# Mixer C's row of scores as one PSUM tile over three banks: one minimum and one exponential for all its keys

## The chip, the cores and the metric

The kernel runs on one core of one Trainium2 chip, as one launch. Its time is the device time of that core in microseconds (us); the figure that counts is the median of the timed runs. A core has TensorE (PE, matrix products into PSUM; loads of its weights are listed apart as PEld), VectorE (DVE), ScalarE (ACT) and GpSimd (POOL) as computing engines, and DMA queues, most of which are fed from SyncE (SP). Each engine takes its instructions in its own order; between engines they wait on semaphores. PSUM is TensorE's output memory, here eight banks of 512 float32 values on each of 128 partitions.

## The reference

The program is one step of a network with two layers over 128 context tokens and 1024 latent tokens, all in float32. The change is in the second layer, whose mixer C is differential attention: each of 8 heads has two query/key maps (z = 0 and 1) of width 64 and values of width 128. A softmax is taken over each map, and the second one, times a number lam, is taken from the first:

```python
def diff_attn_latent(q, k, v, k_ctx, v_ctx, lam):
    ...
    k_all = jnp.concatenate([k_ctx, k], 1)
    v_all = jnp.concatenate([v_ctx, v], 1)
    ...
    def one_block(qblk):
        s = jnp.einsum('bqhzd,bkhzd->bhzqk', qblk, k_all, preferred_element_type=F32) * (C_QK_DIM ** -0.5)
        p = jax.nn.softmax(s, -1)
        att = p[:, :, 0] - lam * p[:, :, 1]
        return jnp.einsum('bhqk,bkhd->bqhd', att.astype(v.dtype), v_all)
```

A latent query block of 128 tokens sees 128 cached context keys and 1024 latent keys, 1152 in all. The 128 context tokens of the other input see one another only: 128 keys. The result goes through a norm, a gate and the output projection.

## The kernel before

Tokens are in nine tiles of 128: tile 0 is the context tokens, tiles 1 to 8 the latent ones. Each float32 operand of most products is split into a high and a low part (hh and hl, wch and wcl, vh and vl, ah and al), and a product is made of two or three matmuls of those parts.

For a head h and a query tile t, `c_probs` (L1539) works on the two maps in turn, and each map's 128 x 1152 scores are called a row of scores here. It makes six matmuls (L1555): three chunks of 384 keys, each a high and a low part of the query. Every chunk has a PSUM tile of its own, one bank, with the tags s0, s1 and s2. VectorE takes each chunk's minimum (the query is scaled by -1/8, so the least value is the largest score; L1557) and the minimum of the three (L1559). ScalarE makes three exponentials with that as bias, each of which also gives the sum over its chunk (L1562; the sum is read by an instruction of its own, ACTIVATION_READ_ACCUMULATOR). After both maps L1571 adds up the three sums, L1573 and L1574 make the factor, and L1575 mixes the two rows into the attention. Tile 0 has one chunk of 128 keys. Between the maps `c_query` (L1528) transposes and splits the next tile's queries.

`c_values` (L1579) later transposes the attention by blocks of 128 keys (L1593), splits it into ah (ScalarE, L1438) and al (VectorE, L1439), and multiplies it with the values (L1603 to L1605).

PSUM is full: two banks each for the pools cpr (projections and gates, tag ps) and ctr (transposes, tag pt), three for csc (the scores, one buffer for each of s0, s1 and s2) and one for cpo (value products). So a chunk's matmuls of the next row can begin when that chunk's exponential of the row before has read its bank. At the end, the output tiles 3, 5 and 7 borrow s0 and s1 as their two banks (p_b, L1851).

What order the work stands in is set in two steps. The program interleaves generators: for every head, rows of scores, value products, the projections of the next head (L360 to L362, `c_project`), gates (L1620 to L1622, `c_gate`) and norms (`c_norm`) are zipped by counts of steps (L1797 and L1804 to L1807). From that a scheduler makes each engine's list by its own estimates of when operands and buffers are free, so a change of instructions also moves others. In the lists a row of scores has the number of its tile (s_19111).

Of the kernel before, what the change touches and what calls it, by code (L numbers as in the profile page):

```python
# [13 lines left out]
AF = mybir.ActivationFunctionType  # L14
ALU = mybir.AluOpType
AX = mybir.AxisListType
# [3 lines left out]
P = 128  # L20
# [3 lines left out]
TOK = NT * P  # L24
# [117 lines left out]
def hybrid_step(ctx: ExitStack, tc: tile.TileContext, I, O, stop=99):  # L142
    nc = tc.nc
    PE, VE, AE, GE, SP = nc.tensor, nc.vector, nc.scalar, nc.gpsimd, nc.sync
# [12 lines left out]
    def tl(pool, shape, tag, dt=F32, bufs=None):  # L157
        uid[0] += 1
        kw = {} if bufs is None else {"bufs": bufs}
        return pool.tile(list(shape), dt, tag=tag, name=f"{tag}_{uid[0]}", **kw)  # L160
# [534 lines left out]
    with ExitStack() as ph1:  # L695
        hp = ph1.enter_context(space("hT0", 1))
        hh, hl = tl(hp, [P, KT, TOK], "hh", F32R), tl(hp, [P, KT, TOK], "hl", F32R)
        with ExitStack() as su:
# [28 lines left out]
            for i in range(3):  # L727
                modulated(i, range(4, KT), thirds[i], xp, pt, hh, hl)
        ap = ph1.enter_context(space("ap", 1))
# [4 lines left out]
        psum = [ph1.enter_context(space(n, b, space=PSUM))  # L734
                for n, b in (("psc", 2), ("ppo", 1), ("ptr", 3), ("ppr", 2))]
        psum = psum[3], psum[2], psum[0], psum[1]
# [535 lines left out]
    with ExitStack() as ph2:  # L1272
# [96 lines left out]
        for i in range(-2, len(items)):  # L1369
# [47 lines left out]
            t = TIMES[min(i + 2, 2) if i < 5 else 3]  # L1417
# [121 lines left out]
    def c_probs(h, t, heads, ap, psum):  # L1539

        p_pr, p_tr, p_s, p_o = psum
        own = t == 0
        nb, w = (1, P) if own else (3, THIRD)
        hd = heads[h]
        if t not in hd.qs:
            c_query(t, hd, ap, psum)
        qs = hd.qs[t]
        p = []
        sums = tl(ap, [P, 2, nb], f"cs{nb}")
        for z in range(2):  # L1550
            s = [tl(p_s, [P, 512], f"s{c}") for c in range(nb)]
            mc, mx = tl(ap, [P, 3], "mc3"), tl(ap, [P, 1], "mx")
            for c in range(nb):
                for e in range(2):
                    PE.matmul(s[c][:, :w], qs[:, e, z], hd.kp[:, z] if own else hd.kst[:, z, w * c:w * c + w],  # L1555
                              start=e == 0, stop=e == 1)
                VE.tensor_reduce(mc[:, c:c + 1] if nb > 1 else mx, s[c][:, :w], axis=AX.X, op=ALU.min)  # L1557
            if nb > 1:
                VE.tensor_reduce(mx, mc, axis=AX.X, op=ALU.min)  # L1559
            e = tl(ap, [P, TOK], "p", bufs=4)  # L1560
            for c in range(nb):
                AE.activation(e[:, w * c:w * c + w], s[c][:, :w], AF.Exp, scale=-1.0, bias=mx,  # L1562
                              accum_out=sums[:, z, c:c + 1])
            p.append(e[:, :nb * w])
            if z == 0:
                h1, t1 = (h, t + 1) if t < 8 else (h + 1, 0)
                if h1 < 8 and t1 in heads[h1].q:
                    c_query(t1, heads[h1], ap, psum)
            yield
        li = hd.sums[:, 2 * t:2 * t + 2]  # L1570
        VE.reduce_sum(li, sums, axis=AX.X)  # L1571
        r = tl(ap, [P, 1], "lr")
        VE.reciprocal(r, li[:, 1:2])  # L1573
        VE.scalar_tensor_tensor(r, r, nlam, li[:, 0:1], op0=ALU.mult, op1=ALU.mult)  # L1574
        VE.scalar_tensor_tensor(p[0], p[1], r, p[0], op0=ALU.mult, op1=ALU.add)  # L1575
        hd.att[t] = p[0]
        yield
# [102 lines left out]
    with ExitStack() as ph3:  # L1680
# [76 lines left out]
        if stop <= 3:  # L1757
# [3 lines left out]
        ap = ph3.enter_context(space("ac", 2))  # L1761
        psum = [ph3.enter_context(space(n, b, space=PSUM))
                for n, b in (("cpr", 2), ("ctr", 2), ("csc", 1), ("cpo", 1))]
# [84 lines left out]
                yield  # L1848

        p_a = lambda: [tl(psum[0], [P, 512], "ps") for _ in range(2)]  # L1850
        p_b = lambda: [tl(psum[2], [P, 512], f"s{i}") for i in range(2)]  # L1851
        banks = [p_a, p_a]

        def first_ready():
# [33 lines left out]
```

## Time and profile before

| | us |
|---|---|
| time, median of 3 runs | 2082.01 |
| lowest and highest run | 2075.63 and 2087.13 |
| span of the profiled execution | 2077.4 |
| scores of mixer C, first to last | 1181 to 1998 |
| six score matmuls of a row, 128 such rows (L1555, 1152 keys) | 196.0 busy |
| chunk minima (L1557, 384 keys) | 204.4 busy |
| exponentials (L1562, those of tile 0 among them) | 225.1 busy |

The page gives the profiled execution's span, from its first to its last instruction, and no device time beside it; the span lies within the range of the three timed runs, 4.6 us below their median. The page has each engine's busy time with its share of the span and its instructions. A window gives the same for a stretch of time, with TensorE's granted clock (PEclk, 1.00 is full). A group's row has the line, the engine, the operation, output<-inputs, the shapes and the count; then the busy time, the mean of one in ns, and the idle time of the engine just before them with what ended it. A row of the waits says who waited for whom, for how long in all, how many times and at most. A row of the timeline has the start, the duration and the instruction, with the idle time ahead of it in brackets.

### The profile page before, as it was taken

What the parts mean: (1) busy time and instruction counts of PE and PEld (TensorE: products, weight loads), DVE (VectorE), ACT (ScalarE), POOL (GpSimd) and SP (SyncE); (2) the same over time, 40 slices, a digit from 0 to 9 for tenths busy, and PEclk for the clock granted to TensorE, in tenths of its full rate; (3) what the DMA queues carried; (4) which work ended last, traced back from release to release, by engine and by line L of the source; (5) the groups of instructions that cost most, each with busy time, mean ns of one, the idle gap of its engine ahead of it and who ended that gap; (6) DMA issues with size and microseconds to landing.
All of it is one profiled execution on the core that took longest, in us unless ns stands there. A gap on an engine that the chain in (4) does not pass through costs nothing. (4 is left out here: it accounts for less than half of the span.)

```text
span 2077.4 us, 40804 instructions
## 1 busy us (share of the span) xinstructions
PE 1952.1 (94%) x15148; PEld 1777.4 (86%) x15148; DVE 1488.3 (72%) x3821; ACT 1058.8 (51%) x2808; POOL 673.6 (32%) x951
## 2 busy tenths in 40 slices
PE   7899999999789999999989999999999999999998
PEld 7899999999678888777768888999998989898786
DVE  5355567565767787877488587878787878787867
ACT  4343345333446555564356554565555555555643
POOL 0222232332167657575043223121312121212204
PEclk9999999999999999999999999999999999999999
DMA  7511133112555454534576401010101010101325
GB/s 290 163 62 65 61 98 115 63 57 78 181 178 158 146 171 148 157 111 129 167 228 218 133 21 45 15 50 10 51 9 55 6 56 5 55 5 49 106 68 177
DMA packets 165079, 205.72 MB, mean 99 GB/s; under 512 B 16368, under 2 KB 108048, under 8 KB 164880
## 3 DMA queue, kind: packets, MB, share of 16 engines
q1 hardware_dynamic: 162016, 198.25, 30.1%
q10 hardware_dynamic: 2864, 4.85, 0.7%
q8 instruction: 120, 1.97, 0.4%
q14 instruction: 79, 0.65, 0.1%
HBM read 152.32 MB, written 50.74 MB: 98 GB/s over the span
## 5 line engine op out<-in xcount | busy, mean ns | idle before, releaser
L1562 ACT ACTIVATE p<-s,mx 128x384 f32<-128x384 f32 (+1 forms) x400 | 225.1, 572 | 123.0 <-DVE mx L1559 100.3
L1557 DVE TENSOR_REDUCE mc<-s 128x1 f32<-128x384 f32 x384 | 204.4, 551 | 29.3 <-PE s L1555 26.2
L1555 PE MATMUL s<-kst,qs 128*128 128x384 f32 x768 | 196.0, 355 | 14.1 <-ACT p L1562 13.6
L360 PE MATMUL ps<-wch,hh 128*128 128x384 f32 x576 | 205.5, 358 | 3.0 <-DMA raw<-in_wgc_dram 0.9
L361 PE MATMUL ps<-wcl,hh 128*128 128x384 f32 x576 | 198.6, 345 | 4.1 <-POOL wcl L271 4.1
L362 PE MATMUL ps<-wch,hl 128*128 128x384 f32 x576 | 196.4, 341 | 0.3 <-DVE hl L1707 0.2
L407 POOL TENSOR_TENSOR q<-ropea,ropeb 128x256 f32<-128x256 f32 x56 | 44.0, 786 | 442.4 <-DVE ropeb L404 302.3
L374 PE MATMUL ps<-hh,wgh 128*128 128x384 f32 x504 | 174.5, 346 | 5.8 <-DVE bo L242 4.3
L376 PE MATMUL ps<-hh,wgl 128*128 128x384 f32 x504 | 172.4, 342 | 0.0
L375 PE MATMUL ps<-hl,wgh 128*128 128x384 f32 x504 | 171.9, 341 | 0.0
L1555 PEld LDWEIGHTS s<-kst,qs 128*128 128x128 f32 x768 | 127.5, 190 | 29.8 <-ACT p L1562 22.4
L271 POOL TENSOR_TENSOR wgl<-raw,wgh 128x1024 fp32r<-128x1024 f32 (+1 forms) x39 | 75.5, 1939 | 234.5 <-ACT wgh L270 234.5
L1083 POOL TENSOR_TENSOR rp<-rp,tmp 128x126 f32<-128x126 f32 (+22 forms) x279 | 130.3, 467 | 21.9
L1081 POOL TENSOR_TENSOR tmp<-mp,rp 128x126 f32<-128x126 f32 (+22 forms) x279 | 117.8, 422 | 52.3 <-DVE mp L1072 31.1
L1438 ACT CAST ah<-pt 128x512 fp32r<-128x512 f32 (+2 forms) x168 | 86.1, 533 | 79.7 <-PE pt L1593 76.3
L1439 DVE TENSOR_TENSOR al<-pt,ah 128x512 fp32r<-128x512 f32 (+2 forms) x168 | 100.6, 615 | 32.1 <-ACT ah L1438 30.8
L360 PEld LDWEIGHTS ps<-wch,hh 128*128 128x128 f32 x576 | 109.6, 191 | 6.5 <-DVE vl L1439 2.4
L361 PEld LDWEIGHTS ps<-wcl,hh 128*128 128x128 f32 x576 | 109.8, 191 | 6.2 <-POOL wcl L271 5.8
L362 PEld LDWEIGHTS ps<-wch,hl 128*128 128x128 f32 x576 | 109.5, 190 | 1.4 <-DVE hl L1707 1.3
L271 POOL TENSOR_TENSOR wcl<-raw,wch 128x512 fp32r<-128x512 f32 x54 | 76.5, 1423 | 84.5 <-ACT wch L270 84.5
L374 PEld LDWEIGHTS ps<-hh,wgh 128*128 128x128 f32 x504 | 95.4, 189 | 8.1 <-DVE bo L242 4.9
L1575 DVE SCALAR_TENSOR_TENSOR p<-p,lr,p 128x1152 f32<-128x1152 f32 (+1 forms) x72 | 98.4, 1367 | 0.4
(463 smaller groups left out, 5721.7 us busy)
## 6 DMA issues: line engine op xcount, KB each, us to landing
hb<-pbT SPq DMA_DIRECT2D x90, 256.0 KB, 3.9
adaw<-in_ada_w_dram SPq DMA_DIRECT2D x56, 256.0 KB, 3.6
raw<-in_wc_dram SPq DMA_DIRECT2D x48, 256.0 KB, 2.7
adaw<-in_ada_w_dram SPq DMA_DIRECT2D x8, 1024.0 KB, 10.9
pbT<-bm SPq DMA_DIRECT2D x16, 512.0 KB, 2.7
low<-lowT SPq DMA_DIRECT2D x16, 512.0 KB, 4.1
raw<-in_wo_dram SPq DMA_DIRECT2D x32, 256.0 KB, 2.8
raw<-in_wpb_dram SPq DMA_DIRECT2D x13, 512.0 KB, 3.4
```

The lines of the kernel that those rows point to most:

```text
L271: eng.tensor_tensor(lo[:, j:j + w], raw[:, :w], hi[:, j:j + w].bitcast(F32), ALU.subtract)
L360: PE.matmul(ps[:, :n], hh[:, k, s], wh[:, k], start=k == 0, stop=False)
L361: PE.matmul(ps[:, :n], hh[:, k, s], wl[:, k], start=False, stop=False)
L362: PE.matmul(ps[:, :n], hl[:, k, s], wh[:, k], start=False, stop=k == KT - 1)
L374: PE.matmul(ps[:, :THIRD], wh[:, k], hh[:, k, s], start=k == 0, stop=False)
L375: PE.matmul(ps[:, :THIRD], wh[:, k], hl[:, k, s], start=False, stop=False)
L376: PE.matmul(ps[:, :THIRD], wl[:, k], hh[:, k, s], start=False, stop=k == KT - 1)
L1081: eng.tensor_tensor(tv, m[:, j - a:j - a + 1, 0:j].to_broadcast([P, n, j]), rpb[:, t:16, j:j + 1].to_broadcast([P, n, j]), ALU.mult)
L1083: eng.tensor_tensor(rpb[:, t:16, 0:j], rpb[:, t:16, 0:j], tv, ALU.add)
L1555: PE.matmul(s[c][:, :w], qs[:, e, z], hd.kp[:, z] if own else hd.kst[:, z, w * c:w * c + w], start=e == 0, stop=e == 1)
L1557: VE.tensor_reduce(mc[:, c:c + 1] if nb > 1 else mx, s[c][:, :w], axis=AX.X, op=ALU.min)
L1562: AE.activation(e[:, w * c:w * c + w], s[c][:, :w], AF.Exp, scale=-1.0, bias=mx, accum_out=sums[:, z, c:c + 1])
```

## The change

The three chunks of a row become one tile of three banks, [128, 3, 512], of which 384 columns of each bank are used. The six matmuls write its banks as before. One minimum over both free dimensions takes the place of the three chunk minima and the minimum of them, one exponential over all 1152 keys takes the place of three, and its sum goes straight into the array of sums, so L1571 is gone. The pool keeps its three banks and one buffer, so the next row's first matmul now follows the whole exponential of the row before. Tile 0's rows take the first 128 columns of such a tile. The output tiles that borrowed s0 and s1 take the first two banks of one such tile.

```diff
-        sums = tl(ap, [P, 2, nb], f"cs{nb}")
+        li = hd.sums[:, 2 * t:2 * t + 2]
         for z in range(2):
-            s = [tl(p_s, [P, 512], f"s{c}") for c in range(nb)]
-            mc, mx = tl(ap, [P, 3], "mc3"), tl(ap, [P, 1], "mx")
+            s, mx = tl(p_s, [P, 3, 512], "s"), tl(ap, [P, 1], "mx")
+            sv = s[:, 0:nb, 0:w]
             for c in range(nb):
                 for e in range(2):
-                    PE.matmul(s[c][:, :w], qs[:, e, z], hd.kp[:, z] if own else hd.kst[:, z, w * c:w * c + w],
+                    PE.matmul(sv[:, c], qs[:, e, z], hd.kp[:, z] if own else hd.kst[:, z, w * c:w * c + w],
                               start=e == 0, stop=e == 1)
-                VE.tensor_reduce(mc[:, c:c + 1] if nb > 1 else mx, s[c][:, :w], axis=AX.X, op=ALU.min)
-            if nb > 1:
-                VE.tensor_reduce(mx, mc, axis=AX.X, op=ALU.min)
-            e = tl(ap, [P, TOK], "p", bufs=4)
-            for c in range(nb):
-                AE.activation(e[:, w * c:w * c + w], s[c][:, :w], AF.Exp, scale=-1.0, bias=mx,
-                              accum_out=sums[:, z, c:c + 1])
-            p.append(e[:, :nb * w])
+            VE.tensor_reduce(mx, sv, axis=AX.XY, op=ALU.min)
+            e = tl(ap, [P, TOK], "p", bufs=4)[:, :nb * w]
+            AE.activation(e.rearrange("p (c n) -> p c n", n=w), sv, AF.Exp, scale=-1.0, bias=mx,
+                          accum_out=li[:, z:z + 1])
+            p.append(e)
...
-        li = hd.sums[:, 2 * t:2 * t + 2]
-        VE.reduce_sum(li, sums, axis=AX.X)
...
-        p_b = lambda: [tl(psum[2], [P, 512], f"s{i}") for i in range(2)]
+        p_b = lambda: [v for v in [tl(psum[2], [P, 3, 512], "s")] for v in (v[:, 0], v[:, 1])]
```

The file is five lines shorter, so lines behind `c_probs` have lower numbers after it: the mixing is L1575 before and L1570 in the change, the gates are L1615 to L1617.

The first place shown is TensorE's list in a middle head, from one row of scores (query tile 2, z = 0) to the next (z = 1). Names are output<-inputs: s is a row of scores, ps a projection or a gate, pt a transpose; x2 is two in a row. Before:

```order
L1555 MATMUL s_3853_19726<-kst_18062,qs_19652 128x384 x2
...
L1555 MATMUL s_3854_19727<-kst_18062,qs_19652 128x384 x2
...
L1555 MATMUL s_3855_19728<-kst_18062,qs_19652 128x384 x2
L362 MATMUL ps_19781<-wch_19375,hl_12965 128x384
...
L1519 MATMUL pt_19805<-cst_61,k_19752 128x128 x2
L1658 MATMUL pt_19810<-cst_61,sq_19677 128x128 x2
L1555 MATMUL s_3865_19762<-kst_18062,qs_19652 128x384 x2
```

And in the change, between the same two rows:

```order
L1555 MATMUL s_19111<-kst_17618,qs_19047 128x384 x6
L360 MATMUL ps_19150<-wch_18783,hh_12964 128x384
...
L1519 MATMUL pt_19173<-cst_61,k_19129 128x128 x2
L1653 MATMUL pt_19178<-cst_61,sq_19072 128x128 x3
...
L1588 MATMUL pt_19199<-cst_61,p_19042 128x128
L1615 MATMUL ps_19223<-hh_12964,wgh_19188 128x384
...
L1555 MATMUL s_19139<-kst_17618,qs_19047 128x384 x6
```

The six matmuls of a row now stand together, where others stood among them before. From the last of one row to the first of the next there were seven projection matmuls and four transposes; now there are twelve projection matmuls, three of a gate and six transposes.

The second place is VectorE's list at the same point, where mc and mx are the minima, lr the factor of the mixing and p the attention. Before:

```order
L1557 TENSOR_REDUCE mc_3856_19729<-s_3854_19727 128x1
L1571 TENSOR_REDUCE sums_18063<-cs_3831_19629 128x2
L1439 TENSOR_TENSOR vl_19404<-ps_19615,vh_19403 128x128
L1573 RECIPROCAL lr_19705<-sums_18063 128x1
L1557 TENSOR_REDUCE mc_3856_19729<-s_3855_19728 128x1
L1574 SCALAR_TENSOR_TENSOR lr_19705<-lr_19705,nlam_5651,sums_18063 128x1
L1559 TENSOR_REDUCE mx_19730<-mc_3856_19729 128x1
L1575 SCALAR_TENSOR_TENSOR p_19645<-p_19697,lr_19705,p_19645 128x1152
```

And in the change:

```order
L1568 RECIPROCAL lr_19091<-sums_17619 128x1
L1569 SCALAR_TENSOR_TENSOR lr_19091<-lr_19091,nlam_5651,sums_17619 128x1
L1570 SCALAR_TENSOR_TENSOR p_19042<-p_19086,lr_19091,p_19042 128x1152
L1557 TENSOR_REDUCE mx_19112<-s_19111 128x1
L1439 TENSOR_TENSOR vl_18812<-ps_19019,vh_18811 128x128
```

The mixing of the tile before stood behind the new row's minimum of three (L1559); in the change it stands ahead of the new row's one minimum.

## The prediction

> **What bounds the kernel now.** I read the page first, then the windows of the part that the change touches, then the waits of TensorE.
>
> ```profile
> span 2077.4 us, 40804 instructions
> PE 1952.1 (94%) x15148; PEld 1777.4 (86%) x15148; DVE 1488.3 (72%) x3821; ACT 1058.8 (51%) x2808; POOL 673.6 (32%) x951
> ...
> core 0: us, PE busy (x) PEld busy (x) DVE busy (x) ACT busy (x) POOL busy (x), PEclk, DMA share, GB/s
> 1182.00:2000.00 818.00, 785.93 (x4870) 728.80 (x4871) 649.33 (x1801) 467.65 (x1387) 190.09 (x184) 0.99 0.12 36
> ...
> 1538.78:1641.83 103.05, 100.03 (x636) 93.92 (x636) 82.34 (x234) 58.42 (x176) 24.03 (x25) 1.00 0.10 31
> 1641.83:1744.67 102.84, 99.95 (x637) 94.08 (x636) 82.35 (x234) 58.42 (x176) 24.04 (x25) 1.00 0.10 30
> ```
>
> Mixer C's scores run from 1182 to 2000 us. There TensorE is busy 785.9 of 818 us, at a granted clock of 0.99: 32.1 us of idle is all that any edit of the other engines can win in this part. VectorE (79%) and ScalarE (57%) have room. The middle heads repeat: two stretches of one head each last 103.05 and 102.84 us and leave TensorE 3.0 us of idle apiece. So the question is not how much VectorE and ScalarE save, but what the change does to these 32 us.
>
> ```profile
> PE s L1555 <- ACT p L1562: 14.0, 19, 1.5
> PE ps L361 <- POOL wcl L271: 4.1, 5, 1.6
> PE po L1605 <- DVE al L1439: 3.3, 9, 1.2
> PE po L1603 <- ACT ah L1438: 2.6, 5, 0.6
> ```
>
> The largest share, 14.0 us in 19 waits, is score matmuls (L1555) waiting for exponentials (L1562) to empty their bank. This is the term that the change acts on.
>
> **Durations.** These groups are from 1500 to 1800 us, but for the last two, which are from 1182 to 2000.
>
> ```profile
> L1562 ACT ACTIVATE p<-s,mx 128x384 f32<-128x384 f32 x144 | 82.2, 581 | 47.5 <-DVE mx L1559 38.3 <-DVE il L1637 8.8
> L1562 ACT ACTIVATE p<-s,mx 128x128 f32<-128x128 f32 x6 | 2.3, 376 | 0.2
> L1557 DVE TENSOR_REDUCE mc<-s 128x1 f32<-128x384 f32 x142 | 75.8, 550 | 6.1 <-PE s L1555 4.9
> L1557 DVE TENSOR_REDUCE mx<-s 128x1 f32<-128x128 f32 x6 | 1.7, 286 | 3.4 <-PE s L1555 3.4
> ...
> L1559 DVE TENSOR_REDUCE mx<-mc 128x1 f32<-128x3 f32 x128 | 19.0, 149 | 1.0
> L1571 DVE TENSOR_REDUCE sums<-cs 128x2 f32<-128x6 f32 (+1 forms) x72 | 11.1, 155 | 28.2 <-ACT p L1562 27.7
> ```
>
> A minimum over 1152 elements isn't in the trace. Its slope is (550 - 286) / 256 = 1.03 ns per element, so 550 + 768 x 1.03 = 1342 ns; at worst it costs its three parts, 1650. The exponential has (581 - 376) / 256 = 0.80 ns, so 581 + 768 x 0.80 = 1196 ns; at worst three parts, 1743. I take 1.34 and 1.20 us, since both shapes read the same bytes as before. VectorE then saves 3 x 550 + 149 - 1342 = 457 ns on each of 128 rows, 58 us, and 11 us of L1571: 70 us of its 649. ScalarE is weighed from one row of scores below.
>
> The Trainium skill, page "ScalarE: Activation LUTs", section "What ACT_TABLE_LOAD costs", gives about 280 ns plus 0.833 ns per element for such an instruction: 1240 ns by estimate. The trace's 581 ns at 384 elements agrees with it (600), and the sum would move by 0.04 us per row.
>
> ```profile
> 1507.00 0.62 PE L1555 MATMUL s<-kst,qs 128*128 128x384 f32 x2 [0.93 <-ACT p L1562]
> ...
> 1508.68 0.51 PE L1555 MATMUL s<-kst,qs 128*128 128x384 f32 x2
> ...
> 1509.39 0.34 PE L361 MATMUL ps<-wcl,hh 128*128 128x384 f32 x1
> 1509.56 0.34 PE L362 MATMUL ps<-wch,hl 128*128 128x384 f32 x1
> ...
> 1510.27 0.38 PE L1519 MATMUL pt<-cst,k 128*128 128x128 f32 x2
> 1510.49 0.38 PE L1658 MATMUL pt<-cst,sq 128*128 128x128 f32 x2
> 1510.74 0.44 PE L1555 MATMUL s<-kst,qs 128*128 128x384 f32 x1
> ```
>
> ```profile
> 1507.80 0.59 ACT L1562 ACTIVATE p<-s,mx 128x384 f32<-128x384 f32 x1
> 1508.28 0.20 ACT L1562 ACTIVATION_READ_ACCUMULATOR p<-s,mx 128x1 f32 x1
> ...
> 1510.02 0.58 ACT L1562 ACTIVATE p<-s,mx 128x384 f32<-128x384 f32 x1 [1.39 <-DVE mx L1559]
> ...
> 1510.59 0.57 ACT L1562 ACTIVATE p<-s,mx 128x384 f32<-128x384 f32 x1
> ...
> 1511.15 0.58 ACT L1562 ACTIVATE p<-s,mx 128x384 f32<-128x384 f32 x1
> 1511.61 0.21 ACT L1562 ACTIVATION_READ_ACCUMULATOR p<-s,mx 128x1 f32 x1
> ```
>
> ```profile
> 1509.10 0.15 DVE L1573 RECIPROCAL lr<-sums 128x1 f32<-128x1 f32 x1
> 1509.23 0.56 DVE L1557 TENSOR_REDUCE mc<-s 128x1 f32<-128x384 f32 x1
> 1509.71 0.21 DVE L1574 SCALAR_TENSOR_TENSOR lr<-lr,nlam,sums 128x1 f32<-128x1 f32 x1
> 1509.84 0.15 DVE L1559 TENSOR_REDUCE mx<-mc 128x1 f32<-128x3 f32 x1
> 1509.95 1.42 DVE L1575 SCALAR_TENSOR_TENSOR p<-p,lr,p 128x1152 f32<-128x1152 f32 x1
> ```
>
> Three exponentials and their sums hold ScalarE from 1510.02 to 1511.82, 1.80 us; one with its read takes about 1.30 by the same overlap. That is 0.5 us on 128 rows, 64 us of 468. All of these savings lie beside TensorE's work.
>
> **What takes their place: the hold of the banks.** Here the row of scores ends at 1508.68 + 0.51 = 1509.19. The last minimum, the minimum of three and the first exponential follow, and the next row's first matmul starts at 1510.74, 1.55 us after the end: it needs bank 0 alone, and banks 1 and 2 are still to be read. With one tile the hold is 0.04 + 1.34 + 0.03 + 1.20 + 0.14 = 2.75 us, hops as in these rows, plus what VectorE has queued ahead of the minimum. No part of the minimum runs under the row's own matmuls any more.
>
> TensorE's cover is the other work between two rows: 0.175 us for a 384-column matmul (1509.39 to 1509.56) and 0.11 for a transpose (1510.27 to 1510.49 for two), less 0.17 by which the last matmul ends after its slot. Counted so in the program's order for a middle head, the sixteen covers before are 2.3, 2.0, 1.5, 2.3, 3.3, 4.5, 5.1, 4.0, 3.5, 4.2, 4.0, 8.3, 3.5, 1.7, 2.0 and 2.3 us. Those of the change are 3.1, 2.9, 3.1, 2.7, 3.6, 4.6, 4.1, 4.0, 3.3, 5.8, 2.9, 9.9, 2.9, 3.3, 3.6 and 2.8: the scheduler has put more work between the tight rows. Nine of them are 3.3 or less.
>
> The queue can be read at the place shown in the section on the change. VectorE's mixing of two rows (L1575, 1.42 us) used to stand behind the minimum of three; now it (L1570) stands ahead of the whole minimum. It is ready 0.09 (the read), 0.15, 0.21 and some 0.2 of hops after the earlier row's exponential, and ends 2.1 us after it. The new row, let in by the same exponential, ends 0.14 + 6 x 0.175 + 0.17 = 1.36 us after it. So the minimum starts 0.74 us late, the hold is 3.5 us, and the cover there, fifteen 384-column matmuls and six transposes, is 3.29 - 0.17 = 3.1: TensorE waits 0.4 us where it waits for nothing now.
>
> **The sum.** With no queue a head's sixteen holds exceed their covers by next to nothing; with 0.4 us on each (3.15 us) by 1.65 us in all; with 0.74 on each (3.49) by 4.4. I take 0.4, since the queue of 0.74 is forced only behind a mixing, every other row, and a cover over 4 gives slack ahead of it. Times eight heads that is 13.2 us (0 to 35), for the 14.0 that go: **-0.8 us** (-14 to +21). Behind a score matmul that waits stand TensorE's projections and value products, so all of such a wait counts. Less load on VectorE and ScalarE shortens the waits for al and ah, 5.9 us: -3; but behind the minimum VectorE has the residuals al (L1439) queued, which L1605 needs, and a minimum of 1.34 us holds them up 0.8 us longer than one of 0.55: on nine such waits 7 us. The bounds are -6 to +7. In the last head two rows stand back to back in both orders and one pair has only 1.6 us between: each gains a wait of about 1.2 us, +2.5. The output tiles at the end use two thirds of the same tile at L1851; its next user starts after another tile's 24 matmuls of 0.389 us each at most, and its last reading, two squares of 0.73 us together, is over long before, so I cost that at nothing; without that cover it would be 0.73 us on each of two tiles. No DMA is added or moved past another by the edit itself. Together -1.3 us on the profiled span of 2077.4. No time of that execution is given beside its span; the median of the three runs is 2082.0, 4.6 us above it, and I add that: **2081 us**.
>
> ```profile
> 2044.08 0.73 ACT s L330 x2
> ...
> L834 PE MATMUL s<-hh,kst x16: 389/389/389, 2036.9 to 2052.6; 128*128 128x512 f32 x16
> ```
>
> **Rivals.** (a) Faster: the queue vanishes with 70 and 64 us less work. The waits for banks fall from 14.0 to 2, and of the other 18 us of idle half goes: -21, 2061 us. For it speaks that VectorE, at 79%, held the minimum of three in most waits of ScalarE (38.3 of 47.5 us); against it, that the mixing now stands ahead of the minimum.
>
> (b) Slower: the hold costs more than the cover everywhere, 4.4 us a head, and a blocked VectorE passes 7 us on: 2082 + 21 + 7 + 2.5, about 2113. It decides once the minimum starts more than some 0.5 us after the row's last matmul on average. The Trainium skill speaks for this rival: "Perfetto Trace Analysis", section "Optimizing Tensor Performance", wants independent matmul groups to rotate through banks so that the reading of one overlaps the next group. By that rule the change gives up a rotation. The trace shows that rotation at work: at 1507.00 a row enters bank 0, 0.8 us before the third exponential begins.
>
> (c) The wide instructions gain nothing over their parts: 1.65 and 1.74 us, a hold of 3.6 before any queue, 4.0 with 0.4. The covers then fall short by 9.8 us a head, 78 in all for the 14 that go: 2146 us.
>
> **How the numbers follow.** The forecast case, about even, has 0.45; (a) and smaller gains 0.29; (b) 0.22 and (c) 0.04, together 0.26. A measurement of this kernel tells 0.5%, 10.4 us, from no change. The range runs from all of (a), 2061, to all of (b), 2113; (c) and a gain beyond (a) are left out. Within it the even case alone spans 2072 to 2092.
>
> **What would show it.** A minimum near 1.34 us and an exponential near 1.20 confirm the sizes; over 1.6 means (c). The wait of L1555 for the exponential should stay between 8 and 22 us; under 4 means (a), over 30 (b). The stretch of a middle head should keep 103 us within 1. VectorE's busy time should fall by 70 us and ScalarE's by 64, or my slopes are wrong. If the span moves while TensorE's idle between 1182 and 2000 us doesn't, the account is wrong altogether.

## The result, and the profile after

The changed kernel takes 2098.30 us, the median of six runs (2095.26 to 2105.59). The kernel before took 2081.56 us in six runs beside it. The ratio on record is **1.0072**, with a 95% interval of 1.0050 to 1.0093: 0.7% slower, some 15 us, outside the half per cent that was called "no change". (The quotient of the two medians is 1.0080; the ratios of this document are those on record.) The profiled execution took 2095.26 us, with a span of 2093.5 us: 16.1 us more than the span of before.

The first lines of the page after:

```profile
span 2093.5 us, 39910 instructions
PE 1960.4 (94%) x15148; PEld 1785.3 (85%) x15148; DVE 1458.1 (70%) x3365; ACT 1001.4 (48%) x2296; POOL 662.3 (32%) x951
```

The groups of after from 1500 to 1800 us, with the mean of one in ns behind the busy time:

```profile
L1557 DVE TENSOR_REDUCE mx<-s 128x1 f32<-128x1152 f32 x47 | 63.7, 1356 | 18.2 <-PE s L1555 17.5
L1559 ACT ACTIVATE p<-s,mx 128x1152 f32<-128x1152 f32 x47 | 57.6, 1225 | 32.7 <-DVE mx L1557 32.7
```

The wide minimum takes 1356 ns and the wide exponential 1225, about what their slopes gave. So the instructions do what the change says, VectorE and ScalarE work less, and the kernel is slower all the same.

**Where the 16 us lie.** Four stretches cover the time from the first score matmul to the end: the first head (with tile 0's rows ahead of it), five middle heads, the last two heads up to the last score matmul, and the rest. Windows of before, then of after:

```profile
1180.90:1293.86 112.96, 104.77 (x620) 96.15 (x620) 85.50 (x233) 61.91 (x187) 31.78 (x30) 0.94 0.12 34
1293.86:1806.17 512.31, 499.11 (x3177) 469.98 (x3176) 412.93 (x1171) 292.18 (x875) 119.07 (x120) 1.00 0.10 31
1806.17:1995.43 189.26, 178.07 (x1059) 159.31 (x1059) 149.36 (x394) 111.00 (x317) 39.24 (x34) 0.99 0.18 54
1995.43:2077.40 81.97, 74.10 (x355) 60.75 (x353) 54.56 (x140) 30.67 (x77) 25.11 (x18) 0.98 0.44 146
```

```profile
1186.38:1296.66 110.28, 102.97 (x620) 94.31 (x620) 80.67 (x175) 55.02 (x123) 28.30 (x30) 0.95 0.12 35
1296.66:1817.21 520.55, 499.54 (x3176) 469.21 (x3176) 392.34 (x886) 255.94 (x555) 113.84 (x120) 1.00 0.10 30
1817.21:2006.09 188.88, 176.14 (x1050) 159.57 (x1050) 140.06 (x283) 95.77 (x191) 38.64 (x34) 0.98 0.18 54
2006.09:2093.50 87.41, 76.55 (x362) 61.68 (x361) 57.35 (x137) 31.22 (x74) 24.99 (x18) 0.96 0.41 137
```

The first head is 2.7 us shorter, the five middle heads are 8.2 longer, the last two 0.4 shorter, the tail 5.4 longer. The remaining 5.5 us are ahead of the first score matmul (1180.9 to 1186.4), in code that the change doesn't touch; the section on the hardware comes back to them. In the middle heads TensorE is busy as long as before (499.5 and 499.1 us), so nearly all of the 8.2 us is idle time: 13.2 becomes 21.0. The last two heads and the tail don't hold the same work: the first of them has nine matmuls fewer than before (1050 for 1059), the tail seven more (362 for 355). In the last two heads idle time grew too, from 11.2 to 12.7 us.

TensorE's waits in the five middle heads, before and after:

```profile
PE s L1555 <- ACT p L1562: 7.3, 12, 1.0
PE po L1603 <- ACT ah L1438: 2.3, 4, 0.6
PE po L1605 <- DVE al L1439: 1.3, 5, 0.3
PE pt L1593 <- DVE p L1575: 0.8, 1, 0.8
```

```profile
PE s L1555 <- ACT p L1559: 10.1, 15, 1.3
PE po L1598 <- ACT ah L1438: 3.1, 5, 0.7
PE pt L1588 <- DVE kst L425: 3.0, 5, 0.6
PE pt L1588 <- DVE p L1570: 2.5, 5, 0.5
PE po L1600 <- DVE al L1439: 1.4, 5, 0.3
```

These rows account for the difference: waits for the banks of the scores grow by 2.8 us, and the others from 4.4 to 10.0. Over half of the others' growth is a wait that before doesn't have in this order: transposes (L1588) waiting for kst (L425), once a head, 0.6 us.

The timeline of after shows where both come from, at the place that the prediction worked out (query tile 2, from the row z = 0 to z = 1) and at the row ahead of it:

```profile
1510.37 1.20 PE L1555 MATMUL s<-kst,qs 128*128 128x384 f32 x6
...
1511.18 1.29 POOL L271 TENSOR_TENSOR wgl<-raw,wgh 128x512 fp32r<-128x512 f32 x1 [1.39 <-ACT wgh L270]
...
1511.50 0.99 DVE L251 SCALAR_TENSOR_TENSOR rst<-rst,vss 128x3 f32<-128x3 f32 x1
...
1513.11 1.36 DVE L1557 TENSOR_REDUCE mx<-s 128x1 f32<-128x1152 f32 x1
...
1514.50 1.22 ACT L1559 ACTIVATE p<-s,mx 128x1152 f32<-128x1152 f32 x1 [1.59 <-DVE mx L1557]
...
1515.86 1.32 PE L1555 MATMUL s<-kst,qs 128*128 128x384 f32 x6 [1.29 <-ACT p L1559]
...
1516.59 1.86 DVE L1570 SCALAR_TENSOR_TENSOR p<-p,lr,p 128x1152 f32<-128x1152 f32 x1
...
1518.38 1.34 DVE L1557 TENSOR_REDUCE mx<-s 128x1 f32<-128x1152 f32 x1
...
1519.75 1.22 ACT L1559 ACTIVATE p<-s,mx 128x1152 f32<-128x1152 f32 x1 [0.89 <-DVE mx L1557]
...
1519.95 0.43 DVE L425 TENSOR_TENSOR kst<-pt,kst 64x256 fp32r<-64x256 f32 x1
...
1520.43 0.33 PE L1588 MATMUL pt<-cst,p 128*128 128x128 f32 x1 [0.61 <-DVE kst L425]
...
1521.12 1.13 PE L1555 MATMUL s<-kst,qs 128*128 128x384 f32 x5
```

The first wait, 1.29 us, is for the banks. The row of query tile 1, z = 1, ends at 1510.37 + 1.20 = 1511.57, and its minimum starts 1.54 us later, because VectorE is in a norm's chain of short instructions. The next row follows 0.14 us after the exponential's end (1515.72 and 1515.86).

The second wait is for kst. The row z = 0 ends at 1515.86 + 1.32 = 1517.18. Its minimum starts 1.20 us later, because VectorE is in the mixing until 1518.4. L425, which gives a bank back to the transposes, is queued behind the minimum of 1.34 us, and TensorE's transpose waits 0.61 us for it. The exponential ends at 1520.97 and the next row starts at 1521.12, 3.9 us after the end of the row ahead of it, with no wait of its own. But that is again 0.15 us after the exponential, as soon as the banks let it in: without the wait for kst TensorE would have come 0.61 us sooner and, by that step, waited there for the banks. So at this place, once in each of the five heads, the wait for kst stands in for one for the banks, and the rows above count the hold too low by up to 3.0 us.

The bank waits of the five heads come at three of a head's sixteen rows only. The first one here makes 5.8 of the 10.1 us; before waits at that row too, 4.5 of its 7.3.

What the prediction didn't see is that some of VectorE's instructions take longer while GpSimd works. L251 took 0.99 us, and 0.16 at 1510.46; it ends at 1512.49, as GpSimd's L271 does (1512.47). The mixing took 1.86 us while GpSimd's L407 ran to 1517.24. From 1190 to 2000 us of after, none of 48 mixings without GpSimd beside them took over 1.42 us, and none of 56 factors (L1569) over 0.22; with it they took up to 1.86 and 1.29. The waits for the mixing (L1570), 0.5 us a head, also stand behind a factor of 0.79 us beside L407. The traces show that the two come together; no run takes GpSimd's work away. Both kernels have this (before's L252 took 1.02 us beside L271 at the same row), so it isn't new with the change; but both late minima shown here stand behind such instructions.

### The profile page after: what moved, and what is told of

The parts are those of the page before. It is cut to its first block, busy times and chain, and to the rows that moved or that the text cites. A ratio compares the mean times of both kernels' runs of the same rounds, so it can differ in the third digit from the quotient of the medians.

```text
span 2093.5 us, 39910 instructions
## 1 busy us (share of the span) xinstructions
PE 1960.4 (94%) x15148; PEld 1785.3 (85%) x15148; DVE 1458.1 (70%) x3365; ACT 1001.4 (48%) x2296; POOL 662.3 (32%) x951
## 5 line engine op out<-in xcount | busy, mean ns | idle before, releaser
L1557 DVE TENSOR_REDUCE mx<-s 128x1 f32<-128x1152 f32 (+1 forms) x144 | 178.1, 1237 | 57.5 <-PE s L1555 55.6
L1559 ACT ACTIVATE p<-s,mx 128x1152 f32<-128x1152 f32 (+1 forms) x144 | 162.7, 1130 | 94.8 <-DVE mx L1557 93.6
L407 POOL TENSOR_TENSOR q<-ropea,ropeb 128x256 f32<-128x256 f32 x56 | 47.3, 845 | 448.4 <-DVE ropeb L404 276.8
L1555 PE MATMUL s<-kst,qs 128*128 128x384 f32 x768 | 171.5, 350 | 17.3 <-ACT p L1559 17.3
L271 POOL TENSOR_TENSOR wgl<-raw,wgh 128x1024 fp32r<-128x1024 f32 (+1 forms) x39 | 74.6, 1917 | 235.3 <-ACT wgh L270 235.3
L1588 PE MATMUL pt<-cst,p 128*128 128x128 f32 x584 | 97.1, 279 | 8.2 <-DVE kst L425 3.7
L271 POOL TENSOR_TENSOR wcl<-raw,wch 128x512 fp32r<-128x512 f32 x54 | 69.2, 1288 | 92.6 <-ACT wch L270 92.3
## 6 DMA issues: line engine op xcount, KB each, us to landing
adaw<-in_ada_w_dram SPq DMA_DIRECT2D x8, 1024.0 KB, 10.6
```

Of the source, the lines that this page charges most:

```text
L271: eng.tensor_tensor(lo[:, j:j + w], raw[:, :w], hi[:, j:j + w].bitcast(F32), ALU.subtract)
L1555: PE.matmul(sv[:, c], qs[:, e, z], hd.kp[:, z] if own else hd.kst[:, z, w * c:w * c + w], start=e == 0, stop=e == 1)
L1557: VE.tensor_reduce(mx, sv, axis=AX.XY, op=ALU.min)
L1559: AE.activation(e.rearrange("p (c n) -> p c n", n=w), sv, AF.Exp, scale=-1.0, bias=mx, accum_out=li[:, z:z + 1])
```

## The experiments

For each run the ratio is to the kernel before on the same chip, with its 95% interval. "Head" is the mean of the five middle heads; "tail" is the time from the last score matmul's end to the end of the last computing instruction, 3 us ahead of the span's end. In most runs a middle head holds 635 matmuls, but in e4 and e7 the list gives the first of the five 612; the mean of the other four stands in brackets.

| run | what it is | ratio | head, us | tail, us |
|---|---|---|---|---|
| b0_before | the kernel before | 1.0008 (0.9998 to 1.0018) | 102.5 | 79.0 |
| a0_change | the change | 1.0072 (1.0050 to 1.0093) | 104.6 | 84.4 |
| e1_tail_other_banks | change, output tiles in other banks | 1.0041 (1.0027 to 1.0055) | 104.5 | 80.6 |
| e2_one_tile_parts | one tile, three minima, three exponentials | 1.1058 (1.1032 to 1.1085) | 131.6 | 73.0 |
| e3_wide_exp | one tile, three minima, one exponential | 1.0802 (1.0778 to 1.0826) | 123.5 | 70.0 |
| e4_wide_min | one tile, one minimum, three exponentials | 1.0068 (1.0050 to 1.0086) | 103.6 (104.4) | 82.7 |
| e8_split_min | change, three minima behind the row | 1.0145 (1.0127 to 1.0163) | 105.7 | 75.7 |
| e9_short_min | change, minimum over 384 keys | 1.0040 (1.0025 to 1.0055) | 103.5 | 84.8 |
| e10_short_exp | change, exponential over 384 keys | 1.0046 (1.0031 to 1.0061) | 103.5 | 84.5 |
| e5_one_and_two | a tile of one bank, then one of two | 1.0056 (1.0039 to 1.0074) | 104.1 | 79.3 |
| e7_two_and_one | a tile of two banks, then one of one | 0.9980 (0.9968 to 0.9992) | 101.4 (101.9) | 79.9 |
| o5_before | before, another order | 1.0021 (1.0003 to 1.0040) | 103.8 | 77.5 |
| o5_change | change, the same other order | 1.0094 (1.0071 to 1.0117) | | |
| o8_before | before, a third order | 1.0017 (1.0001 to 1.0033) | 103.3 | 82.0 |
| o8_change | change, the third order | 1.0067 (1.0048 to 1.0085) | 104.0 | 85.4 |

Tails compare only between kernels with much the same list up to there: in e2, e3 and e8 the last head is so much longer (97 to 115 us to its last score matmul, for 89 in the change) that work of the tail is done by then.

### The change and the kernel before once more

> The change once more, beside the kernel before on one chip. If the 5.5 us that its profile lost ahead of mixer C (the same code and order) were chance in the granted clock, that part differs this time by another amount, under 3 us either way, and the ratio falls to about 1.005. If the change somehow slows that part, it is 5 us again. Middle heads 104.1 us against 102.5, tail (from the last score matmul) 84.4 against 79.1.

> The kernel before again, for a second profile beside the others: the granted clock ahead of mixer C decides by chance, so its start of mixer C lies anywhere from 1181 to 1192 us, and its middle heads (102.5 us on the mean) and its tail (79 us) repeat within 0.5 us. Ratio 1.000 within its interval.

The result repeats, and so do the stretches: heads of 102.5 and 104.6 us, tails of 79.0 and 84.4. The first head, 2.7 us shorter in the first pair, is 0.1 shorter in this one, so that gain is no part of the account. Two things came out otherwise than expected: the ratio didn't fall to 1.005, and the part ahead of mixer C is 3.1 us longer in the change (1188.7 and 1191.8 us), just over the 3 set for chance. From the first score matmul on, the change's span is 16.3 us longer in this pair, and 10.6 in the first.

### The tail: output tiles that share one tile

```diff
-        p_b = lambda: [v for v in [tl(psum[2], [P, 3, 512], "s")] for v in (v[:, 0], v[:, 1])]
+        p_b = lambda: [tl(psum[1], [P, 512], "pt") for _ in range(2)]
```

> The change, but the output tiles 3, 5 and 7 take two tiles of one bank from the transposes' pool and not two thirds of the score tile. Theory 'shared tile': the tail goes from 84.4 back to 79 to 80 us and the ratio to the change is 5 us better; heads stay at 104.1. Rival 'late order': the tail grew because the work around it was put in another order, and stays at 83 or more.

The ratio falls from 1.0072 to 1.0041, and the heads stay as long. Windows of after, of before and of this run, each from the first matmul of the borrowed banks to the end:

```profile
2049.06:2093.50 44.44, 33.80 (x145) 26.61 (x143) 29.61 (x68) 13.94 (x37) 18.17 (x13) 0.93 0.51 177
```

```profile
2036.87:2077.40 40.53, 32.91 (x145) 26.85 (x143) 27.81 (x68) 13.62 (x37) 18.27 (x13) 0.96 0.56 192
```

```profile
2052.09:2092.70 40.61, 32.91 (x145) 26.85 (x143) 27.86 (x68) 13.61 (x37) 18.27 (x13) 0.93 0.55 189
```

The stretch with these 145 matmuls takes 3.9 us longer in the change, and with two separate tiles it takes what it took before. The timeline of after shows the wait; a half of an output tile is 12 matmuls here:

```profile
2049.06 0.39 PE L834 MATMUL s<-hh,kst 128*128 128x512 f32 x1
...
2051.78 0.39 PE L834 MATMUL ps<-hh,vl 128*128 128x512 f32 x1
...
2054.74 0.60 ACT L330 ACTIVATE s<-hl 128x512 f32<-128x512 f32 x1 [2.84 <-DVE hl L841]
...
2055.52 0.50 PE L834 MATMUL s<-hh,kst 128*128 128x512 f32 x1 [0.82 <-ACT s L330]
```

And of before, the same two halves of s:

```profile
2036.87 0.39 PE L834 MATMUL s<-hh,kst 128*128 128x512 f32 x1
...
2039.59 0.39 PE L834 MATMUL s<-hh,kst 128*128 128x512 f32 x1
...
2042.54 0.60 ACT L330 ACTIVATE s<-hl 128x512 f32<-128x512 f32 x1 [2.83 <-DVE hl L841]
```

Before, the second half follows the first at once, 3 us ahead of the first half's square (L330), which writes its unused squares into the bank it has just finished with. After, the second half waits for that square, although it writes another bank: the program orders instructions by tile, and both halves are now parts of one tile. The list is made for that too: halves of s and ps alternate. Three tiles wait so, 0.82, 0.32 and 1.07 us; the rest of the 3.9 is 0.9 us more of busy TensorE and 0.8 more behind its last matmul. **This part is shown**: 3.9 of the tail's 5.4 us. The other 1.5 stay in e1 as well (80.6 for 79.0). They are work that the new list puts behind the last row, not waiting: from the last row's end to the first matmul of the borrowed banks TensorE is busy 42.75 of 42.97 us with 218 matmuls in after (42.74 in e1), and 41.19 of 41.44 with 212 in before.

### Parts of one tile

```diff
-            s = [tl(p_s, [P, 512], f"s{c}") for c in range(nb)]
+            st = tl(p_s, [P, 3, 512], "s")
+            s = [st[:, c] for c in range(nb)]
```

> One tile of three banks, but three chunk minima, the minimum of three and three exponentials as before: the hold is then 0.55 + 0.15 + 1.71 + 0.2 = 2.6 us, with no long minimum. Theory 'hold': middle heads at 104 us or more, as in the change, with about 2 us of waits of L1555 for the exponential per head. Rival 'blocked VectorE' (the 1.36 us minimum delays what stands behind it): middle heads at 102.5 to 103. Tail 84 by the shared tile.

This is the code of before with its three banks in one tile, which the output tiles share as in the change. The second one is the change with a minimum after each chunk's matmuls:

```diff
+                VE.tensor_reduce(mc[:, c:c + 1] if nb > 1 else mx, sv[:, c], axis=AX.X, op=ALU.min)
+            if nb > 1:
+                VE.tensor_reduce(mx, mc, axis=AX.X, op=ALU.min)
-            VE.tensor_reduce(mx, sv, axis=AX.XY, op=ALU.min)
```

> One tile, chunk minima and the minimum of three as before, one exponential over 1152 keys: hold 0.55 + 0.15 + 1.22 + 0.2 = 2.1 us. Theory 'hold': middle heads between the two, about 103. Rival 'blocked VectorE': 102 to 102.5, since ScalarE is relieved and VectorE has only short minima. Tail 84 by the shared tile.

Both are far slower than I expected: 8 and 11% slower than before. The timeline of e2 shows why:

```profile
1501.34 0.51 PE L1556 MATMUL s<-kst,qs 128*128 128x384 f32 x2
...
1501.95 0.55 DVE L1558 TENSOR_REDUCE mc<-s 128x1 f32<-128x384 f32 x1
...
1502.56 0.61 PE L1556 MATMUL s<-kst,qs 128*128 128x384 f32 x2
```

The first chunk's matmuls end at 1501.85, and the second's wait until the first's minimum is done (1502.50), which reads another bank of the same tile. So these two runs don't measure the hold of the banks, as they were meant to; they show the rule of the tail a second time. They also say something of the change: in one tile a minimum over a part can't run under the row's own matmuls, so the three-bank tile leaves only a minimum behind the row.

### Is it the hold alone?

From the change, with three exponentials again (the hold grows by about 0.5 us, and the minimum stays):

```diff
-            AE.activation(e.rearrange("p (c n) -> p c n", n=w), sv, AF.Exp, scale=-1.0, bias=mx,
-                          accum_out=li[:, z:z + 1])
+            for c in range(nb):
+                AE.activation(e[:, w * c:w * c + w], sv[:, c], AF.Exp, scale=-1.0, bias=mx,
+                              accum_out=sums[:, z, c:c + 1])
```

> The change, but three exponentials of 384 keys for the one of 1152, and their sums added up as before: the banks are held 0.5 us longer (1.36 + 1.71 us), and VectorE has the same long minimum. Theory 'hold': some nine tight rows a head wait up to 0.5 us more each, so middle heads go from 104.1 to 106 or more. Theory 'blocked VectorE': the minimum is what costs, so heads stay within 0.5 us of 104.1.

And with three minima behind the row, each of which lets VectorE's queue go on after 0.55 us:

```diff
-            VE.tensor_reduce(mx, sv, axis=AX.XY, op=ALU.min)
+            for c in range(nb):
+                VE.tensor_reduce(mc[:, c:c + 1] if nb > 1 else mx, sv[:, c], axis=AX.X, op=ALU.min)
+            if nb > 1:
+                VE.tensor_reduce(mx, mc, axis=AX.X, op=ALU.min)
```

> The change, but after all six matmuls three chunk minima and the minimum of three instead of the one wide minimum, and one wide exponential: the banks are held 0.44 us longer (1.65 + 0.15 for 1.36), while VectorE can put other work between the short minima. Theory 'hold': middle heads 105 to 107. Theory 'blocked VectorE': below 104, toward 102.5, and the waits of the transposes for L425 and the mixing go.

Neither theory holds alone. With a longer hold e4's heads of 635 matmuls are 104.4 us, as long as the change's (104.1 and 104.6); "hold" expected 106 or more. With shorter pieces on VectorE e8's are 105.7, where "blocked VectorE" expected less than 104; but they run from 104.5 to 108.4, with 630 to 638 matmuls, and the two with 635 take 104.5 again. TensorE's waits in e4's five heads begin so:

```profile
PE po L1601 <- ACT ah L1438: 7.8, 5, 1.9
PE s L1556 <- ACT p L1561: 5.9, 10, 1.0
```

The bank wait is 5.9 us, below the 10.1 of the change, but the value products now wait 7.8 for ah, which ScalarE makes. Each edit changes the list as well, as the counts of matmuls show, so neither run changes the hold or the minimum alone; a wait that shrinks in one place comes up in another.

### Any shorter hold?

The minimum, and then the exponential, over the last 384 keys only:

```diff
-            VE.tensor_reduce(mx, sv, axis=AX.XY, op=ALU.min)
+            VE.tensor_reduce(mx, sv[:, nb - 1], axis=AX.X, op=ALU.min)
```

> The change, but the minimum is over the last 384 keys alone (it leaves out the other 768): 0.55 us for 1.36, so the banks are held for 0.55 + 1.22 + 0.2 = 2.0 us and VectorE is freed of 0.8 us a row. Theory 'minimum behind the row' (the long minimum, which cannot start before the sixth matmul, is what costs): middle heads fall to 102.5 or below. Theory 'any hold': the same as the next run, which holds the banks as long.

```diff
-            AE.activation(e.rearrange("p (c n) -> p c n", n=w), sv, AF.Exp, scale=-1.0, bias=mx,
+            AE.activation(e[:, nb * w - w:], sv[:, nb - 1], AF.Exp, scale=-1.0, bias=mx,
                           accum_out=li[:, z:z + 1])
+            if nb > 1:
+                GE.memset(e[:, :nb * w - w], 0.0)
```

> The change, but the exponential is over the last 384 keys alone and GpSimd writes zeros for the other 768 (it leaves out two thirds of the exponentials): the banks are held for 1.36 + 0.58 + 0.2 = 2.1 us, with the long minimum as in the change. Theory 'minimum behind the row': middle heads stay within 0.7 us of 104.1. Theory 'any hold': 102.5 or below, as the run before.

Both give heads of 103.5 us, so in these two runs it doesn't matter on which engine 0.6 to 0.8 us of the hold go. (e10 isn't the shorter hold alone: with its memsets GpSimd is busy for 165 us of the five heads, 114 in the change.) The 102.5 that both theories expected of e9, and "any hold" of e10, didn't come. They win only 0.6 to 1.1 us of the 1.6 to 2.1 by which the heads had grown, with 0.6 us off each of sixteen holds. The waits for kst vanish in both; those for the mixing grow, from 2.5 us in five heads to 4.7 in e9 and 4.0 in e10.

### Two tiles

From the change, a row in a tile of two banks and one of one bank, so that one minimum runs under the row's own matmuls again. First one bank, then two:

```diff
-            s, mx = tl(p_s, [P, 3, 512], "s"), tl(ap, [P, 1], "mx")
+            s0, s1 = tl(p_s, [P, 512], "s0"), tl(p_s, [P, 2, 512], "s1") if nb > 1 else None
+            sv = [s0[:, :w], *((s1[:, 0, :w], s1[:, 1, :w]) if nb > 1 else ())]
...
+                if c == 0:
+                    VE.tensor_reduce(mc[:, 0:1] if nb > 1 else mx, sv[0], axis=AX.X, op=ALU.min)
+            if nb > 1:
+                VE.tensor_reduce(mc[:, 1:2], s1[:, :, :w], axis=AX.XY, op=ALU.min)
+                VE.tensor_tensor(mx, mc[:, 0:1], mc[:, 1:2], ALU.min)
...
-        p_b = lambda: [v for v in [tl(psum[2], [P, 3, 512], "s")] for v in (v[:, 0], v[:, 1])]
+        p_b = lambda: [tl(psum[2], [P, 512], "s0"), tl(psum[2], [P, 2, 512], "s1")[:, 0]]
```

> A row in two tiles the other way round: chunk 0 in a tile of one bank, chunks 1 and 2 in one of two. The wider minimum (0.95 us) now stands behind the row, and bank 0 comes free after the shorter exponential, so the next row enters after 0.95 + 0.15 + 0.58 + 0.2 = 1.9 us, as in the run with two and one (1.8). By 'minimum behind the row' middle heads are 0.5 to 1.5 us longer than that run's 101.4; by 'release in two steps' they are the same within 0.4. Tail 79 to 80 in both.

Then two banks first, with the minimum over both under the third chunk's matmuls and the exponential over both ahead of the single one:

```diff
+            sv = [s1[:, 0, :w], s1[:, 1, :w], s0[:, :w]] if nb > 1 else [s0[:, :w]]
...
+                if c == 1:
+                    VE.tensor_reduce(mc[:, 1:2], s1[:, :, :w], axis=AX.XY, op=ALU.min)
+            VE.tensor_reduce(mc[:, 0:1] if nb > 1 else mx, s0[:, :w], axis=AX.X, op=ALU.min)
```

> A row in two tiles: chunks 0 and 1 in one of two banks with one minimum and one exponential, chunk 2 in one of one bank; the output tiles take a bank of each. The wider minimum runs beside chunk 2's matmuls, and the next row enters after 0.55 + 0.15 + 0.9 + 0.2 = 1.8 us. By 'hold' middle heads are at 102.5 or below, by 'shared tile' the tail is at 79 to 80, and the whole is within 0.5% of the kernel before or faster. If wide instructions on two banks cost as the one on three does, by 'blocked VectorE', heads stay near 104.

e7 beats both kernels: 0.2% faster than before, its interval short of 1, and 0.9% faster than the change (0.998 / 1.0072). The minimum over two banks, from the groups from 1500 to 1800 us, and TensorE's waits in the five middle heads:

```profile
L1561 DVE TENSOR_REDUCE mc<-s 128x1 f32<-128x768 f32 x48 | 45.8, 955 | 17.7 <-PE s L1558 17.3
```

```profile
PE s L1558 <- ACT p L1567: 4.4, 10, 0.6
PE pt L1598 <- DVE p L1580: 4.2, 5, 0.8
```

Without the first head, which has fewer matmuls, the bank waits are 3.3 us, less than the 5.9 of before in the same four heads, and a head has 101.9 us for 102.6. The gain of 0.2% is no larger than what another order alone does to before (1.0017 and 1.0021, below). e5 has the same instructions in the other sequence, and 104.1: 2.2 us more, where the theories expected 0.5 to 1.5 or less than 0.4. From the row's end to the first exponential's end both are worked out alike, about 0.55 + 0.15 + 0.90 = 1.60 us in e7 (a minimum over one bank, the minimum of two, an exponential over two banks) and 0.95 + 0.15 + 0.58 = 1.68 in e5; what differs is that e5 has the long minimum behind the row and the long exponential last. Which of the two counts, and how much of the 2.2 us the list adds, the runs don't tell.

By the Trainium skill, page "Perfetto Trace Analysis", section "Optimizing Tensor Performance", independent groups of matmuls should rotate through banks, so that one is emptied under the next. e7 agrees as to the sign, 0.9980 with two tiles for 1.0072 with one. e5, at 1.0056 with two tiles as well, can't be told from one tile, and three tiles (before) are not better than e7's two.

### The order by itself

The lists differ between before and after, so I gave both kernels two other lists, by one number at L1678 (L1673 in the change):

```diff
-        return zipped(c_values(C_GROUPS[g], heads[h], ap, psum), 1 + (NT if g else 1), nxt, 6 if g1 else 3)
+        return zipped(c_values(C_GROUPS[g], heads[h], ap, psum), 1 + (NT if g else 1), nxt, 5 if g1 else 3)
```

and the same with 8 in place of 6.

> The kernel before with the same altered number, 5 steps for 6. Theory 'the tile': middle heads near 102.5, at least 1 us below the run beside it. Theory 'the order': off 102.5 by 1 us or more, and no fixed distance to the run beside it.

> The change with one number of the interleaving altered (value products against rows of scores: 5 steps for 6), so the same instructions in another order. Theory 'the tile': middle heads stay 1 us or more above those of the kernel before with the same number. Theory 'the order': they scatter by 1 us or more against 104.1, either way.

> The kernel before with 8 steps for 6. Theory 'the tile': middle heads near 102.5. Theory 'the order': off by 1 us or more, without a fixed distance to the run beside it.

> The change with 8 steps for 6. Theory 'the tile': middle heads 1 us or more above the next run's. Theory 'the order': scatter by 1 us or more against 104.1.

With each number the change is slower than before with the same number: 1.0072 with 6, 1.0094 / 1.0021 = 1.0073 with 5, 1.0067 / 1.0017 = 1.0050 with 8. But the order alone makes a head of before 0.8 to 1.3 us longer, as large as most of what is to be explained; with 8 the heads differ by 0.6 us only (103.3 and 104.0), less than the 1 us of theory "the tile". The order alone also brings the wait for kst: in the five heads of o5_before, with its short minima, transposes wait 5.1 us for it, longer than in the change (3.0). The profiled execution of o5_change took 4533 us in place of 2101, so no head or tail is read from it.

## Why the prediction was wrong

The forecast was 2081 us and no change; it came out at 2098, on rival (b)'s side and inside the range. Two terms of the sum failed, the tail and the relief of the other waits, and a third, the bank waits, had the wrong size and sign.

**Right: the sizes.** 1.34 and 1.20 us were forecast, 1.36 and 1.23 came. The savings are half right: ScalarE's busy time fell by 57 us on the page (64 forecast), VectorE's by 30 (70). The durations of VectorE's minima and sums do add up to 61 us less (204.4 + 19.0 + 11.1 before, 173.5 after), but the short minima had overlapped their neighbours (in the prediction's own rows one starts 0.08 us ahead of the end of another), so the sum of durations was not busy time. Nothing hung on it.

**Failed: "I cost that at nothing".** This was the step on the output tiles, whose "next user starts after another tile's 24 matmuls". It asked who uses the tile next, and not who uses the other part of it meanwhile: the tile's own second half, which the program now holds back until the first half's square. Measured: 3.9 us, and taken out by e1. The alternative named there, 0.73 us on each of two tiles, was a wait for squares too, but of the tile's next user. The squares that count are those of the tile's own first half, in three tiles.

**Failed: the sign of the relief.** "Less load on VectorE and ScalarE shortens the waits for al and ah", −3 us, with +7 as the bound. In five middle heads the waits other than those for the banks grew from 4.4 to 10.0 us. The step had named the mechanism, a minimum of 1.34 us that holds up what is queued behind it, but for al alone; that wait is unchanged (1.3 to 1.4). In this list it was kst (L425) that stood behind the minimum, and the transposes that waited for its bank, 3.0 us. I followed one of the instructions behind the minimum and not all. How much of this is the wide minimum's doing is open: o5_before has the wait without it, and at the place shown it only stands in for a wait for the banks.

**Mis-sized: the bank waits.** "−0.8 us" by 1.65 us a head; in the middle heads they are 2.0 (10.1 / 5), where before had 1.5. The hold itself was right: where nothing stands ahead of the minimum, the exponential ends 2.65 us after the row, and with the 0.14 to the next row's matmul that is 2.8 (2.75 forecast). The queue was taken as 0.4 us on each of nine tight rows; only three rows of a head wait. At the place shown the queue was 1.20 us and not 0.74, since the factor took 0.51 us there and not 0.21 and the mixing 1.86 and not 1.42, beside GpSimd. Over all heads the bank waits are 18.9 us for the 14.0 of before, +4.9 where −0.8 was forecast, but within the 8 to 22 that the prediction allowed. The wait of after, from 1182 to 2020 us:

```profile
PE s L1555 <- ACT p L1559: 18.9, 23, 2.8
```

**Not seen as such: the last head.** "+2.5" was expected; the last two heads are 0.4 us shorter, but with nine matmuls fewer. Their idle time grew by 1.6 us, so a part of the wait may be there.

**Right side, too high a price: rival (b).** The minimum stands behind the mixing, TensorE waits for banks, and a blocked VectorE passes it on, as (b) said; but the price of 2113 came from 4.4 us of bank waits a head, and 2.0 were measured, or 2.6 with the waits for kst that stand in for them.

The last sign named, that TensorE's idle time between 1182 and 2000 us must move with the span, holds for the middle heads, where nearly all of the growth is idle. Another, that a middle head keeps 103 us within 1, failed narrowly: 104.1 and 104.6. The last sign says nothing of the tail, which lies behind 2000 us.

**Open.** Of the 1.6 to 2.1 us by which a middle head grew, the share of the long hold, of the new list, and of where GpSimd's work now falls. The runs show that a shorter hold returns 0.6 to 1.1, and that new lists alone move before's heads by 0.8 to 1.3; no run has the change's instructions in the old list, and none takes GpSimd's work away.

## What to carry to other kernels

When buffers are merged into one tile, look for every pair of instructions that used to touch different ones: where the program keeps order by tiles, parts of one tile serialize, within its own group as well as between groups. Here wider instructions took 57 us of work off ScalarE and 30 off VectorE, engines with room to spare, and won nothing; they turned pipelined pieces into one block, and what is queued behind such a block must be followed one by one. Where fewer and wider instructions are wanted, the best split here let the wide reading run under the last part of the writing (e7: two banks and one). And when a scheduler remakes the list with every edit, count the matmuls of a stretch before its time is compared, and try other orders of both kernels.

## What the runs showed of the hardware

TensorE's granted clock falls to half for a few us at a time in the part ahead of mixer C, partly at other moments in each execution. Two stretches of 3.4 us of after, one behind the other, with the clock third from the end of the row, and two of before at the same place in the work, 3.4 us earlier:

```profile
797.00:800.40 3.40, 2.32 (x34) 1.80 (x32) 3.37 (x9) 1.32 (x3) 1.40 (x5) 1.00 0.74 229
800.40:803.80 3.40, 3.40 (x26) 3.28 (x25) 2.02 (x4) 2.34 (x4) 1.82 (x3) 0.50 0.30 85
```

```profile
793.60:797.00 3.40, 2.32 (x34) 1.87 (x32) 3.33 (x9) 1.58 (x4) 1.44 (x5) 1.00 0.70 214
797.00:800.40 3.40, 3.40 (x41) 3.15 (x40) 2.85 (x7) 2.45 (x5) 2.03 (x4) 1.00 0.37 98
```

Both have the same 34 matmuls and a wait of 1.08 us (L1049 for L1040) in the first stretch; the clock falls after it in the one execution and not in the other.

Over the 317 such stretches from 100 to 1180 us, 3.4 us times one less the clock adds up to 17 us in before, 29 in after, 31 in b0_before and 34 in a0_change. Their first score matmuls follow the same sequence: 1180.9, 1186.4, 1188.7 and 1191.8 us. TensorE's 9944 matmuls ahead of mixer C are the same in before and after, in the same order. So 5.5 of the profile's 16.1 us are no work of the change, and one profile of each kernel would have misled; the timed ratio is what counts. The clock isn't all of it: e5 lost 27 us so and starts at 1180.8, as early as before.

Waiting can cost more than the wait. In e2's five middle heads TensorE is busy 563.7 us, for 499.1 before, with the same matmuls, at a clock of 0.90. The window of these heads, and three stretches of 3.4 us in it, one after the other:

```profile
1321.88:1979.86 657.98, 563.73 (x3178) 497.10 (x3176) 425.76 (x1171) 293.85 (x875) 114.12 (x120) 0.90 0.08 24
...
1538.40:1541.80 3.40, 2.11 (x11) 1.43 (x9) 2.17 (x7) 0.40 (x1) 0.00 (x0) 1.00 0.01 2
1541.80:1545.20 3.40, 1.24 (x4) 0.59 (x4) 1.83 (x5) 1.40 (x6) 0.00 (x0) 1.00 0.00 0
1545.20:1548.60 3.40, 2.75 (x12) 2.71 (x13) 2.20 (x4) 1.17 (x2) 0.00 (x0) 0.51 0.00 0
```

After two stretches with TensorE busy 2.1 and 1.2 us of 3.4, the third is granted half the clock. The Trainium skill, page "TensorE: Matmul & The Clock Gate", section "What's actually happening", describes such a gate, which halves the clock after about 3.4 us of too little work; these rows agree as far as they go: half the clock follows the stretch of 1.24 us, and not yet that of 2.11. The change itself stays clear of it: its middle heads keep 1.00.
